# Sets of three dense phases kept in DRAM as high and low parts, and four smaller edits, in a one-core decoder layer

## The chip, the cores and the metric

The kernel runs on one core of a Trainium2 chip. The metric is device microseconds of one execution, the median of three runs. A comparison with another kernel is made on the same chip, and a difference under 0.2% is taken as none that could be told from noise.

The core has five engines that the text names: PE (matmul, with its weight loads PEld), DVE (elementwise, reads PSUM), ACT (elementwise and the activation functions, reads PSUM), POOL (elementwise, on SBUF alone) and SP, which issues DMAs. Each engine works off its own list in order, so an instruction that waits holds up all that stands behind it. POOL and ACT can issue DMAs too.

## The reference

One layer of a decoder trunk on x of 2048 tokens by 1024 channels, float32:

```python
mod = silu(c) @ w_ada + b_ada;  shift, scale, gate = split(mod, 3)
u = x * (1 + scale) + shift
q, k, v, a_gate, p_in, p_gate, m_a, m_p = split(u @ w_in)
a = sliding_window_sink_attention(q, k, v) * silu(a_gate) @ w_attn_proj      # 16 heads, window 128
p = group_linear(multiscale_causal_pool(p_in)) * pool_scale * silu(p_gate) @ w_pool_proj
y = (sigmoid(m_a) * a + sigmoid(m_p) * p) @ w_out * (1 + gate)
out = layer_norm(ALPHA * x + y) * ln_gain + ln_bias
```

The pool takes means over the last 2, 4, 8 or 16 tokens, by channel group, less the token itself. Dense products make up nearly all of the arithmetic.

## The kernel before, in words

**Dense products.** Every large product is done with seven block products in place of eight (a Strassen-like scheme on 2 x 2 blocks). A `Quad` (line 226) is a pair of weight tiles with its consumer; `front` (299) and `back` (309) run the seven products of a quad. The moving operand is a *set*: seven named blocks `B11, T1, T2, B21, T3, B22, T4` (and `B12`, which replaces `T2` once the quads are done). To get float32 precision, each operand is split into a high part `hi` (fp32r, a copy by ACT) and a low part `lo = x - hi` (a subtraction by DVE, helper `low`, line 122), and each 128x128 by 128x512 block takes three matmuls (`mm3`), so one product is 12 matmuls. A set tile in SBUF holds `[hi, lo]`, 2 MB for each name. The weights of a quad pass through `W` tiles (2 buffers): POOL forms their sums (lines 240 to 250), ACT and DVE split them (`pair_split` 270, `half_split` 276) into `w_set` tiles (4 buffers).

**Stages, in order.** (1) `head` (941): the modulation vectors, and the sets of u for the first 1024 tokens. (2) `first_phase` (1032): the product with w_in (k, v and the four gates, 17 quads in 9 groups), with side work between the products: folding of the pool weights, spreading of the relative bias, and the sums that make the sets of u for the other 1024 tokens (`sums_to` 189). (3) `attention` (555) for the first half, 64 steps plus a tail; a step computes scores, softmax, transposes and values of two heads by 128 queries, and 12 matmuls of the q or pool projection stand between. (4) `second_phase` (1065): as (2) for the second half; its side work makes the sets of w_out. (5) attention for the second half. (6) the dense phases `attn, pool, attn, pool` of the two halves and then `out` with the layer norm.

**Where sets come from.** `set_store` (109) keeps the blocks of a set in DRAM as plain float32. `build` (181) loads half a block to a `spare` tile and splits it with ACT and DVE into the set; `PLAN` (379) and `planned` (384) say at which position of a dense phase each build stands, the last ten halves of the next phase's set in the last group of the phase before it. At the end of an attention (from step 57 on, `spots`, line 695) sixteen quarter blocks of B11, T2, B21 and B22 of the next dense phase are loaded (`raw`) and split; T1 came earlier (steps 26 to 45). After an attention T3 and T4 are built at once.

**Order.** `ring` (350) calls `tick` after each product; `steps` (369) puts side work at numbered ticks. Instructions that are issued through `pe, act, dve, pool, sp` (class `Ordered`, line 49) stay behind whatever was written before them on their engine. Those issued through `nc.<engine>` are placed by a planner that knows only estimated costs and arrival times. Attention's loop is ordered by hand but for its loads; head, side work and the dense products are left to the planner.

**Stores of attention.** `finish` (621) multiplies an output tile with its gate on POOL, forms the sums T1 to T4 there, and `put` (186) stores each by a DMA that POOL issues. `pool_diff` (614) writes the pool difference by DVE to a tile `pl` with one buffer, which POOL then reads.

Of the kernel before, what the change touches and what calls it, by code (L numbers as in the profile page):

```python
# [18 lines left out]
P = 128  # L19
# [3 lines left out]
CH = 512  # L23
# [35 lines left out]
def kernel(  # L59
# [52 lines left out]
    u_d = [set_store(f"u{s}") for s in range(2)]  # L112
    wo_d = set_store("wo")
# [67 lines left out]
    def build(ph, name, half, store, source=None):  # L181
        r = ph.spare()
        nc.sync.dma_start(r, store[source or name][half].rearrange("p a b -> p (a b)"))
        split_set(name, 2 * half, r.rearrange("p (a b) -> p a b", a=2), 2)

    def put(store, name, i, src):
        nc.gpsimd.dma_start(store[name][i // 2, :, i % 2, :], src)

    def sums_to(store, i, take, load, work, b12, stretch):

        b = []

        def x(r, c):
            return b[r][:, c * CH : (c + 1) * CH]

        def fetch():
            b.extend((take(), take()))
            for r in range(2):
                load(b[r], r)

        def sub(out, a, c):
            nc.gpsimd.tensor_tensor(x(*out), x(*a), x(*c), ALU.subtract)

        def plain():
            for r in range(2):
                for c in range(2):
                    if b12 or (r, c) != (0, 1):
                        put(store, f"B{r + 1}{c + 1}", i, x(r, c))

        return [  # L210
            (stretch * at, f)
            for at, f in (
                (0, fetch),
                (2, lambda: [work(t, r) for r, t in enumerate(b)]),
                (3, plain),
                (7, lambda: sub((0, 1), (0, 1), (0, 0))),
                (8, lambda: (put(store, "T1", i, x(0, 1)), sub((1, 1), (1, 1), (0, 1)))),
                (9, lambda: (put(store, "T2", i, x(1, 1)), sub((1, 0), (1, 0), (1, 1)))),
                (10, lambda: (put(store, "T4", i, x(1, 0)), sub((0, 0), (1, 1), (0, 0)))),
                (11, lambda: put(store, "T3", i, x(0, 0))),  # L220
            )
        ]
# [3 lines left out]
    class Quad:  # L226
# [7 lines left out]
        def load(self, ph, own):  # L234
            self.w, self.a22 = ph.weights(), ph.last(own)
            x = self.w
            nc.sync.dma_start(x[:, 2, :], self.srcs[1][:, 0:CH])
            nc.sync.dma_start(self.a22, self.srcs[1][:, CH:])
            nc.sync.dma_start(x[:, 0, :], self.srcs[0][:, 0:CH])
            nc.gpsimd.tensor_tensor(x[:, 1, :], x[:, 2, :], self.a22, ALU.add)  # L240

        def mid(self):
            x = self.w
            nc.gpsimd.tensor_tensor(x[:, 1, :], x[:, 1, :], x[:, 0, :], ALU.subtract)  # L244
            nc.gpsimd.tensor_tensor(x[:, 2, :], x[:, 0, :], x[:, 2, :], ALU.subtract)  # L245
            nc.sync.dma_start(x[:, 0, :], self.srcs[0][:, CH:])
# [23 lines left out]
    def pair_split(ph, raw):  # L270
        hi, lo = ph.split(), ph.split()
        nc.scalar.copy(by_two(hi), raw)  # L272
        low(nc.vector, by_two(lo), raw, by_two(hi))
        return halves(hi, lo)
# [109 lines left out]
    def planned(hooks, ph, store, last, skip=()):  # L384
        for p, name, half in PLAN:
            if name in skip or (p < 14) != last:
                continue
            key = (-1, p) if last else (0, p - 14)
            hooks.setdefault(key, []).append(lambda name=name, half=half: build(ph, name, half, store))
# [116 lines left out]
    def bias_rows(ph):  # L506
        rel = ph.t.tile([HEADS, BUCKETS], F32, tag="c", bufs=ph.bufs["c"], name="rel")
        nc.scalar.dma_start(rel, relT)
# [15 lines left out]
    def spread_bias(j):  # L524
        nc.scalar.dma_start(e_rep[:, 2 * j : 2 * j + 2, :], e_d[2 * j : 2 * j + 2, :].partition_broadcast(P))
# [29 lines left out]
    def attention(ph, s, q0, nxt):  # L555
# [4 lines left out]
        def ld(name, src, x=None):  # L560
            x = tp.tile([P, CH], F32, tag="ld", bufs=3, name=name) if x is None else x
            nc.sync.dma_start(x, src)
            return x

        def from_bias(name):
            return tp.tile([P, CH], F32, tag="bt", bufs=2, name=name)
# [30 lines left out]
        def pool_sums(m, t, acc):  # L597
# [7 lines left out]
            while k < w:  # L605
                nx = tp.tile([P, 16 + CH], F32, tag="nxt", bufs=2, name="nxt")
# [7 lines left out]
        def pool_diff(m, cur, acc):  # L614
            pl = tp.tile([P, CH], F32, tag="pl", bufs=1, name="pl")
            dve.scalar_tensor_tensor(pl, cur[:, 16:], 1.0 / POOL_W[m // 2], acc, ALU.mult, ALU.subtract)
            return pl

        kept = {}

        def finish(kind, store, m, t, src, gate):
# [4 lines left out]
            if (half, t) == (0, 0):  # L626
                put(store, "B11", i, x)
                return
            if (half, t) == (0, 1):
                pool.tensor_tensor(x, x, kept[kind, 0, 0], ALU.subtract)  # L630
                put(store, "T1", i, x)
                return
            if (half, t) == (1, 0):
                put(store, "B21", i, x)
                return
            put(store, "B22", i, x)
            b11, t1, b21 = kept[kind, 0, 0], kept[kind, 0, 1], kept[kind, 1, 0]
            pool.tensor_tensor(t1, x, t1, ALU.subtract)
            put(store, "T2", i, t1)
            pool.tensor_tensor(b21, b21, t1, ALU.subtract)  # L640
            put(store, "T4", i, b21)
            pool.tensor_tensor(b11, t1, b11, ALU.subtract)
            put(store, "T3", i, b11)
# [51 lines left out]
        spots = {57: (0,), 58: (1, 2), 59: (3,), 60: (4, 5), 61: (6,), 62: (7, 8), 63: (9,), 64: (10, 11), 65: (12, 13), 66: (14,), 67: (15,)}  # L695
        raws, pre = {}, {}

        def spot(x):
            return ("B11", "T2", "B21", "B22")[x // 4], x % 4
# [6 lines left out]
        def early_lo(x, which):  # L706
            hi, lo = pre[x, which]
            low(dve if x or which else pool, by_two(lo), nxt_group[x].first(), by_two(hi))
            (nxt_group[x].late if which else nxt_group[x].mid)()
# [499 lines left out]
```

## Time and profile before

| | |
|---|---|
| median of 3 runs | 1950.37 us (1948.66 to 1953.11) |
| the profiled execution, its own time | 1956.69 us |
| its span, first to last instruction | 1954.6 us |
| PE busy | 1767.0 us (90%) |
| DVE, POOL, ACT busy | 1332.4, 1036.4, 940.2 us |
| mean granted TensorE clock | 0.964 |
| DMA | 320.5 MB, 164 GB/s on average |

The profiled execution lies 0.3% above the median. PE is the engine to watch: with nothing in its way one product of 12 matmuls takes 2.72 us, so time in which PE is idle, or runs at a lower clock, is what can be won or lost. Rows of the trace read: start, duration, engine, line, operation, output <- inputs, count, and in brackets the idle time before with what ended it. In a group's row the last part is the busy time, the mean of one in ns, and the idle time before. SPq, POOLq and ACTq are DMA issues.

### The profile page before, as it was taken

The page shows a single profiled execution, that of the slowest core. Times are in us where ns is not written, and L with a number is a line of the kernel's source. Part 1 is how long each engine was busy: PE and PEld are TensorE (multiplying, and loading weights), DVE is VectorE, ACT ScalarE, POOL GpSimd, SP SyncE. Part 2 cuts the span into 40 slices and gives each one's busy share as a digit, 9 for nine tenths or more (in the row PEclk, how much of TensorE's full clock was granted, in tenths as well). Part 3 has the DMA queues.
Part 4 walks back from the last instruction along what each step waited for, and adds up shares of the span by engine and source line. Part 5 has one row for each costly group of instructions (what it writes and reads, how often), then busy time and mean ns, then how long its engine had stood idle before and what let it go on. Part 6 is the DMA issues. An engine that isn't in the chain of part 4 may idle for free. (4 is left out here: it accounts for less than half of the span.)

```text
span 1954.6 us, 25013 instructions
## 1 busy us (share of the span) xinstructions
PE 1767.0 (90%) x8248; PEld 1457.9 (75%) x8248; DVE 1332.4 (68%) x2226; ACT 940.2 (48%) x1945; POOL 1036.4 (53%) x902
## 2 busy tenths in 40 slices
PE   3789898999999987989999999999779989989996
PEld 3677777778888876767888888887657768767775
DVE  4775756444787778666543467866877897878776
ACT  2533333334777766523333377776634333333443
POOL 5453545451467677665433136567753764566442
PEclk9789999999999999989999999999889999999998
DMA  7463636464344444564332425443466575675432
GB/s 265 182 204 108 221 124 221 142 203 135 114 151 146 141 140 160 192 206 158 123 120 102 153 86 157 135 141 124 145 226 218 187 246 173 221 241 180 139 137 91
DMA packets 134226, 320.48 MB, mean 164 GB/s; under 512 B 17857, under 2 KB 21969, under 8 KB 134097
## 3 DMA queue, kind: packets, MB, share of 16 engines
q1 hardware_dynamic: 109472, 242.80, 38.5%
q0 software_dynamic: 19232, 62.95, 8.4%
q10 hardware_dynamic: 5392, 13.14, 1.9%
q8 instruction: 65, 1.06, 0.2%
q14 instruction: 65, 0.52, 0.1%
HBM read 213.94 MB, written 108.03 MB: 165 GB/s over the span
## 5 line engine op out<-in xcount | busy, mean ns | idle before, releaser
L55 PE MATMUL mm<-set_B,w_set 128*128 128x512 f32 x3240 | 814.9, 401 | 32.5 <-DVE w_set L123 17.5
L55 PEld LDWEIGHTS mm<-set_B,w_set 128*128 128x128 f32 x3240 | 613.5, 192 | 166.5 <-DVE w_set L123 23.5
L55 PE MATMUL lg<-set_T,w_set 128*128 128x512 f32 x2088 | 535.9, 407 | 69.1 <-DVE w_set L123 31.6
L55 PEld LDWEIGHTS lg<-set_T,w_set 128*128 128x128 f32 x2088 | 402.2, 196 | 178.1 <-DVE w_set L123 46.8
L123 DVE TENSOR_TENSOR w_set<-W,w_set 128x1024 fp32r<-128x1024 f32 x166 | 238.8, 1438 | 168.8 <-ACT w_set L272 164.7
L272 ACT CAST w_set<-W 128x1024 fp32r<-128x1024 f32 x166 | 174.0, 1048 | 269.1 <-PE mm L55 188.2
L55 PE MATMUL mm<-set_T,w_set 128*128 128x512 f32 x1080 | 271.6, 400 | 0.0
L55 PEld LDWEIGHTS mm<-set_T,w_set 128*128 128x128 f32 x1080 | 205.7, 193 | 43.1
L250 POOL TENSOR_TENSOR W<-W 128x512 f32<-128x512 f32 x58 | 79.6, 1373 | 177.3 <-DVE w_set L123 167.0
L244 POOL TENSOR_TENSOR W<-W 128x512 f32<-128x512 f32 x58 | 95.9, 1654 | 146.6 <-DVE w_set L123 130.6
L323 POOL TENSOR_TENSOR p<-p,u 128x512 f32<-128x512 f32 x58 | 85.8, 1482 | 104.5 <-DVE u L322 104.3
L55 ACT ACTIVATE L<-L,nm 128x257 f32<-128x257 f32 (+1 forms) x256 | 127.1, 498 | 7.9 <-DVE nm L55 2.8
L55 DVE TENSOR_TENSOR o<-pv,o 64x128 f32<-64x128 f32 x256 | 71.9, 281 | 79.4 <-ACT o L55 76.8
L240 POOL TENSOR_TENSOR W<-W,A 128x512 f32<-128x512 f32 x58 | 85.6, 1475 | 63.1 <-DMA W<-in_win_dram 20.9
L55 DVE CUSTOM_DVE_ANT_0 L<-lg,bt,nsink 128x256 f32<-128x256 f32 (+1 forms) x256 | 111.6, 473 | 5.3 <-PE lg L55 1.3
L55 ACT ACTIVATE L<-L,sm 128x256 f32<-128x256 f32 (+1 forms) x128 | 64.3, 502 | 81.2 <-DVE sm L55 81.2
L245 POOL TENSOR_TENSOR W<-W 128x512 f32<-128x512 f32 x58 | 93.4, 1611 | 9.9 <-DMA W<-in_win_dram 3.8
L55 POOL TENSOR_TENSOR w_set<-W,w_set 128x1024 fp32r<-128x1024 f32 x16 | 38.4, 2402 | 102.4 <-ACT w_set L55 69.3
L55 PE MATMUL pv<-pth,vv 128*128 128x256 f32 x248 | 69.6, 297 | 25.5 <-ACT pth L55 21.7
L123 DVE TENSOR_TENSOR w_set<-A,w_set 128x512 fp32r<-128x512 f32 x58 | 86.1, 1516 | 5.4 <-ACT w_set L279 5.3
L123 DVE TENSOR_TENSOR set_T<-spare,set_T 128x1024 fp32r<-128x1024 f32 (+1 forms) x48 | 67.0, 1398 | 32.8 <-ACT set_T L178 32.5
L55 DVE TENSOR_SCALAR L<-L,sm 128x256 f32<-128x256 f32 (+1 forms) x128 | 87.6, 684 | 0.0
(174 smaller groups left out, 2577.3 us busy)
## 6 DMA issues: line engine op xcount, KB each, us to landing
W<-in_win_dram SPq DMA_DIRECT2D x102, 256.0 KB, 3.5
w_set<-wmix_d SPq DMA_DIRECT2D x32, 512.0 KB, 5.5
A<-in_win_dram SPq DMA_DIRECT2D x34, 256.0 KB, 3.8
ag_d<-sig SPq DMA_DIRECT2D x32, 256.0 KB, 3.4
pg_d<-sig SPq DMA_DIRECT2D x32, 256.0 KB, 3.3
ma_d<-sig SPq DMA_DIRECT2D x32, 256.0 KB, 2.6
mp_d<-sig SPq DMA_DIRECT2D x32, 256.0 KB, 2.9
ag<-ag_d SPq DMA_DIRECT2D x32, 256.0 KB, 2.8
```

Source lines behind the costliest of these rows:

```text
L55: return lambda *args, **kw: self.tc.keep_in_program_order(op(*args, **kw))
L123: engine.tensor_tensor(dst, src, as32(hi), ALU.subtract)
L240: nc.gpsimd.tensor_tensor(x[:, 1, :], x[:, 2, :], self.a22, ALU.add)
L244: nc.gpsimd.tensor_tensor(x[:, 1, :], x[:, 1, :], x[:, 0, :], ALU.subtract)
L245: nc.gpsimd.tensor_tensor(x[:, 2, :], x[:, 0, :], x[:, 2, :], ALU.subtract)
L250: nc.gpsimd.tensor_tensor(x[:, 0, :], x[:, 0, :], x[:, 1, :], ALU.subtract)
L272: nc.scalar.copy(by_two(hi), raw)
L323: nc.gpsimd.tensor_tensor(p5, p5, u2, ALU.add)
```

## The change

What it does, part by part:

1. Three set stores, `u1` (u of the second half), `wo` (w_out) and `ain0` (attention output of the first half), hold each block as its high and low part (`split_store`, 2 MB for a name in place of 1 MB). Side work makes the parts: `kept_parts` copies by ACT, subtracts by DVE into two `c` tiles (5 buffers, shared with the gates' `sig` and others) and stores both by SP. `sums_to` does this for u1 (32 times, in `first_phase`) and wo (28 times, in `second_phase`); its POOL subtractions stand 1.5 ticks apart. `resplit` reads the 14 halves that attention stored plainly for `ain0`, splits them (28 times) and stores the parts again, in `second_phase`. Attention of the second half still stores plain blocks, and so does the pool.
2. Where these sets are used, `fill_set` loads a half (1 MB) by one DMA into the set, with no split: T1 in attention at steps 26 and 42, B11, B21, T2 and B22 at steps 57, 58, 59 and 61, T3 and T4 at the start of the next phase, and all fourteen halves of the out phase.
3. The head is written out in a fixed order on all engines. Loads of a tile stand a stage ahead, the spreading of the bias and the folding are ordered at their ticks, and the sets T3, T4 and B22 of the last two blocks are made inside the first phase (`rest`).
4. `pool_diff` writes in place of the pool's sum; the `nxt` tiles have three buffers, and the difference and its gate's multiplication stand one step earlier.
5. Attention's stores are issued by SP, one step after they were called for (`later`).

The diff, cut to its core:

```diff
+    def split_store(name):
+        return {n: dp.tile([4, P, 2, CH], F32, name=f"{name}_{n}_split") for n in set_names}
+    b12_d = dp.tile([2, P, 2, CH], F32, name="b12_d")
+    u1_d = split_store("u1")
+    wo_d = split_store("wo")
+    ain0_d = split_store("ain0")
...
+    def fill_set(name, half, src, eng=None):
+        dst = as32(sets[name][:, 2 * half : 2 * half + 2])
+        (eng or nc.sync).dma_start(dst, src[2 * half : 2 * half + 2].rearrange("i p h c -> p i h c"))
+
     def put(store, name, i, src):
-        nc.gpsimd.dma_start(store[name][i // 2, :, i % 2, :], src)
+        sp.dma_start(store[name][i // 2, :, i % 2, :], src)
+
+    def kept_parts(ph, dst, src):
+        t = []
+        def split():
+            t.extend(ph.c(n, F32R) for n in ("k_hi", "k_lo"))
+            act.copy(t[0], src())
+            low(dve, t[1], src(), t[0])
+        def keep():
+            for h in range(2):
+                sp.dma_start(dst[:, h, :], as32(t[h]))
+        return split, keep
...
+        todo = [(0, fetch), (3, lambda: work(b[0], 0)), (3.5, lambda: work(b[1], 1))]
+        todo += [(at, sub(*z)) for at, z in (
+            (7.5, ((0, 1), (0, 1), (0, 0))), (9, ((1, 1), (1, 1), (0, 1))),
+            (10.5, ((1, 0), (1, 0), (1, 1))), (12, ((0, 0), (1, 1), (0, 0))))]
+        for at, name, z in (
+            (4, "B11", (0, 0)), (4.7, "B12", (0, 1)), (5.4, "B21", (1, 0)), (6.1, "B22", (1, 1)),
+            (8.5, "T1", (0, 1)), (10, "T2", (1, 1)), (11.5, "T4", (1, 0)), (13, "T3", (0, 0)),
+        ):
+            if b12 or name != "B12":
+                split, keep = kept_parts(ph, store[name][i], lambda z=z: x(*z))
+                todo += [(at, split), (at + 1, keep)]
+        return sorted(todo, key=lambda t: t[0])
+
+    def resplit(ph, name, half):
+        r = []
+        def fetch():
+            r.append(ph.spare())
+            sp.dma_start(r[0], ain_d[0][name][half].rearrange("p a b -> p (a b)"))
+        todo = [(0, fetch)]
+        for j in range(2):
+            split, keep = kept_parts(ph, ain0_d[name][2 * half + j], lambda j=j: r[0][:, j * CH : (j + 1) * CH])
+            todo += [(3 + j, split), (4 + j, keep)]
+        return todo
...
         def pool_diff(m, cur, acc):
-            pl = tp.tile([P, CH], F32, tag="pl", bufs=1, name="pl")
-            dve.scalar_tensor_tensor(pl, cur[:, 16:], 1.0 / POOL_W[m // 2], acc, ALU.mult, ALU.subtract)
+            pl = cur[:, 16:]
+            dve.scalar_tensor_tensor(pl, pl, 1.0 / POOL_W[m // 2], acc, ALU.mult, ALU.subtract)
...
+            for what in puts:
+                put(*what)
+            puts.clear()
...
+            if n in (59, 62):
+                nxt_group[n // 62].mid()
...
             if n in (26, 42):
-                t1_raw = ph.weights()[:, 0:2]
-                nc.sync.dma_start(t1_raw, nxt_store["T1"][n // 42])
-            if n in (29, 45):
-                split_set("T1", 2 * (n // 45), t1_raw, 2, eng=(act, pool))
+                fill_set("T1", n // 42, nxt_store["T1"], sp)
+            for start, name in ((57, "B11"), (58, "B21"), (59, "T2"), (61, "B22")):
+                if n == start:
+                    for half in range(2):
+                        fill_set(name, half, nxt_store[name], sp)
...
-            for x in spots.get(n, ()):
-                name, i = spot(x)
-                split_set(name, i, raws.pop(x), eng=(act, dve))
...
+        load_w(0)
+        load_x(0)
+        load_w(4)
+        load_x(4)
+        for q in grp:
+            q.load(ph, False, sp, pool)
+        load_w(1)
+        modulation(0)
+        load_x(1)
+        sets_a(0)
...
+        products(2)
+        sets_a(3)
+        sets_b(3)
+        products(3)
+        return groups, turn, opened, cb, lambda: (sets_c(2), sets_c(3))
...
-            steps(hooks, groups, 9 + 24.5 * i, todo)
+            steps(hooks, groups, 5 + 26.5 * i, todo)
+            for n in range(4):
+                if halves_of:
+                    steps(hooks, groups, 19 + 26.5 * i + 2.6 * n, resplit(ph, *halves_of.pop(0)))
...
-                    hooks.setdefault((0, p), []).append(lambda name=name, half=half: build(ph, name, half, ain_d[0]))
+                    hooks.setdefault((0, p), []).append(lambda name=name, half=half: fill_set(name, half, ain0_d[name]))
```

In the head, `sets_a(i)` makes B11 and T1 of block i, `sets_b(i)` B21 and T2, `sets_c(i)` B22, T3 and T4; `load_w` and `load_x` issue the loads of the modulation's weights and of x, and `products(i)` are the first 12 matmuls on block i.

More of the change, by code (lines that the diff above doesn't have):

```diff
@@ L201, in sub @@
         def sub(out, a, c):
[L202 to L222, printed above, removed]
+            return lambda: pool.tensor_tensor(x(*out), x(*a), x(*c), ALU.subtract)
+        todo = [(0, fetch), (3, lambda: work(b[0], 0)), (3.5, lambda: work(b[1], 1))]
+        todo += [(at, sub(*z)) for at, z in (
+            (7.5, ((0, 1), (0, 1), (0, 0))),
+            (9, ((1, 1), (1, 1), (0, 1))),
+            (10.5, ((1, 0), (1, 0), (1, 1))),
+            (12, ((0, 0), (1, 1), (0, 0))),
+        )]
+        for at, name, z in (
[16 more added lines that the diff above has]
+        return todo
     class Quad:
@@ L626, in finish @@
             if (half, t) == (0, 0):
-                put(store, "B11", i, x)
+                later(store, "B11", i, x)
                 return
@@ L694, in attention @@
         seconds = {}
[L695 to L699, printed above, removed]
+        pre = {}
         def early_hi(x, which):
@@ L1010, in head @@
-        groups, turn = gate_quads(0)
-        fetch(0)
-        fetch(4)
-        for q in groups[0]:
-            q.load(ph, False)
-        starts = [pair_split(ph, q.first()) for q in groups[0]]
-        for q in groups[0]:
-            q.mid()
-        opened = [(bank(), bank(), None, None) for q in groups[0]]
-        for i in range(4):
-            make_sets(i)
-            if i + 1 < 4:
-                fetch(i + 1)
-                fetch(i + 5)
+                act.activation(x, x, AF.Identity, bias=mod[:, k : k + 1], scale=mod[:, m : m + 1])
@@ L1024, in head, with products @@
+        opened = [(bank(), bank(), None, None) for q in grp]
+        def products(i):
             for w, (a, b, _, _) in zip(starts, opened):
```

275 lines of the change are left out of this document (157 added, 118 removed).

## The prediction

> **What bounds the kernel now.** I read the page's head first, then busy time by stage, then the chain of waits of PE in the stages with a gap, and at last the timeline there. Columns of the second fence: stretch in us, its length, PE, PEld, DVE, ACT and POOL busy, granted clock, DMA share, GB/s.
>
> ```profile
> span 1954.6 us, 25013 instructions
> PE 1767.0 (90%) x8248; PEld 1457.9 (75%) x8248; DVE 1332.4 (68%) x2226; ACT 940.2 (48%) x1945; POOL 1036.4 (53%) x902
> ```
>
> ```profile
> 0.00:85.00 85.00, 43.45 (x176) 37.68 (x176) 49.76 (x90) 33.67 (x49) 45.63 (x66) 0.89 0.68 239
> 85.00:480.00 395.00, 366.01 (x1626) 298.05 (x1627) 222.10 (x237) 143.07 (x207) 174.23 (x159) 0.96 0.51 172
> 480.00:700.00 220.00, 217.60 (x1240) 189.86 (x1240) 169.18 (x508) 165.75 (x499) 132.18 (x127) 1.00 0.41 131
> 700.00:778.00 78.00, 61.08 (x292) 48.66 (x291) 60.28 (x134) 46.69 (x123) 57.69 (x53) 0.91 0.45 149
> 778.00:960.00 182.00, 165.06 (x679) 132.75 (x680) 121.78 (x118) 67.85 (x97) 106.89 (x93) 0.94 0.52 176
> 960.00:1125.00 165.00, 165.00 (x730) 136.67 (x729) 69.80 (x76) 61.27 (x87) 50.88 (x36) 1.00 0.38 126
> 1125.00:1340.00 215.00, 212.97 (x1219) 186.15 (x1218) 158.91 (x488) 162.87 (x479) 124.37 (x115) 1.00 0.41 130
> 1340.00:1439.00 99.00, 71.36 (x351) 57.68 (x350) 69.17 (x154) 54.45 (x146) 70.53 (x64) 0.89 0.46 152
> 1700.00:1790.00 90.00, 77.14 (x312) 59.43 (x311) 74.43 (x59) 31.39 (x37) 62.17 (x48) 0.96 0.71 234
> ```
>
> PE bounds the kernel: in the middle of both attentions and in 960-1125 it has next to no idle time and a clock of 1.00, so nothing done there for another engine can pay. Length less PE busy gives the idle time that the change can reach: head 41.6 us, first phase 29.0, end of the first attention 16.9, second phase 16.9 (all of it before 960), end of the second attention 27.6, start of the out phase 12.9.
>
> **The head (part 3).**
>
> ```profile
> 28.91 1.53 DVE L123 TENSOR_TENSOR set_T<-b,set_T 128x512 fp32r<-128x512 f32 x1
> 41.17 1.24 ACT L992 ACTIVATE spare<-spare,mod 128x1024 f32<-128x1024 f32 x1 [10.20 <-DMA spare<-in_xt_dram]
> e_rep<-e_d ACTq DMA_DIRECT2D x8, 384.0 KB, 5.9
> spare<-in_xt_dram SPq DMA_DIRECT2D x5, 512.0 KB, 6.9
> ```
>
> Block 0's sets end at 30.4 and ACT waits 10.2 us for block 1's x; its DMAs stood behind others on SP, and eight spreads of the bias ran on ACT's queue meanwhile. In the new order block 1's x is among the first loads and the spreads come at later ticks: -10 us. The splits moved to `rest` lie beside the first products of `back`, which has its own T2 and B21 by then. The fixed order costs something where a load waits: `load_x(2)` needs the `spare` that `sets_c(0)` frees, and the loads of blocks 6 and 3 stand behind it on SP. The trace has no such wait, so I bound it by one landing of 6.9 us at each of blocks 1 to 3, which is 21 us; against it stands at most the 10.2 and one spread (5.9). **Head: -10** (-16 to +11), near the row because the order names the very load that it waited for.
>
> **The ends of the attentions (parts 2, 4, 5).** The first fence groups DVE's work in 1340-1439, the second has waits of PE in 1340-1400 and in 1400-1450, the third is the timeline with two groups of POOL's.
>
> ```profile
> L55 DVE TENSOR_TENSOR set_B<-raw,set_B 128x512 fp32r<-128x512 f32 x12 | 15.7, 1320 | 4.6 <-ACT set_B L55 4.5
> L55 DVE TENSOR_TENSOR set_T<-raw,set_T 128x512 fp32r<-128x512 f32 x4 | 5.1, 1284 | 2.9 <-ACT set_T L55 2.9
> L55 DVE SCALAR_TENSOR_TENSOR pl<-nxt,mm 128x512 f32<-128x512 f32 x4 | 2.7, 683 | 10.1 <-POOL p L55 8.8 <-POOL nxt L55 1.2
> ```
>
> ```profile
> PE pv L55 <- ACT pth L55: 8.6, 3, 6.8
> PE mm L55 <- ACT u L313: 9.3, 1, 9.3
> ```
>
> ```profile
> 1359.04 0.57 POOL L187 DMA_DIRECT2D ain_T<-a  x1 [2.88 <-issue]
> 1369.93 0.69 DVE L55 SCALAR_TENSOR_TENSOR pl<-nxt,mm 128x512 f32<-128x512 f32 x1 [8.84 <-POOL p L55]
> 1371.89 0.58 PE L55 MATMUL pv<-pth,vv 128*128 128x256 f32 x1 [6.83 <-ACT pth L55]
> 1378.74 0.28 PE L55 MATMUL pv<-pth,vv 128*128 128x256 f32 x1
> 1438.04 0.58 ACT L313 COPY u<-mm 128x512 f32<-128x512 f32 x1 [8.67 <-DMA ain_T<-a]
> L187 POOL DMA_DIRECT2D ain_T<-a x32 | 18.1, 566 | 14.0 <-POOL a L55 8.6 <-issue 5.1 <-PE mm L55 0.3
> L187 POOL DMA_DIRECT2D pin_T<-p x32 | 18.0, 563 | 9.5 <-POOL p L55 8.0 <-PE pv L55 0.9 <-PE pt L55 0.3
> ```
>
> Three things hold PE. Sixteen splits take 20.8 us of DVE and 7.5 us of waiting for their casts, inside DVE's softmax list; by loading halves ready they go. The single `pl` buffer makes DVE wait 8.8 us for a late POOL, and softmax, transposes and PE (6.83) wait behind it; written in place, that wait is gone, and what is late next is the pool's sum itself (1.2 us here). POOL is late because it issues the stores: the two rows are 64 of the 112 that the code issues, with 36.1 us busy and 23.5 idle ahead, so some 0.9 us each, 52 us of POOL an attention, which SP takes over at no cost to PE as long as POOL is in time. The last wait, 9.3 us, is `back`'s copy waiting for a store of `a` to land before its memory is reused; without splits and stores ahead of it POOL's last four products come sooner, but a tail stays.
>
> What it costs: SP waits for POOL at each store, with bias tiles, q weights and gates queued behind it. Weights are loaded four steps ahead of use, but a pool gate is now used one step after its load. Fills are 8 DMAs of 1 MB; the stretch 1700-1790 moves 234 GB/s at a share of 0.71, so 330 at full share, 25 us for all. From step 57 to the end of the tail are eleven steps of some 4.2 us (1219 matmuls at 24 a step in 215 us), so B22 is in time; a gate queued behind two fills is 6 us late. Of 44.5 us idle I leave 7 for each end and count nothing for the clock: **-30**. Bounds: all idle but 2 each and the lost clock, -42; only `pl` and a third of the rest, -12.
>
> On the clock: after the 6.83 us gap the same matmul took 0.58 us, later 0.28. [...]
>
> **The out phase (part 2).**
>
> ```profile
> L123 DVE TENSOR_TENSOR set_T<-spare,set_T 128x1024 fp32r<-128x1024 f32 x8 | 12.9, 1615 | 10.0 <-ACT set_T L178 10.0
> L123 DVE TENSOR_TENSOR set_B<-spare,set_B 128x1024 fp32r<-128x1024 f32 x6 | 11.7, 1996 | 0.2 <-ACT set_B L178 0.2
> PE lg L55 <- DVE w_set L123: 6.1, 3, 3.4
> PE lg L55 <- DVE w_set L123: 4.3, 3, 3.4
> ```
>
> All fourteen builds of w_out stand in 1700-1790: 24.6 of DVE's 74.4 us, and the two rows (1700-1750 and 1750-1800) show PE waiting for weights split late on that DVE. As fills they cost DMA alone, 7 MB more at a share of 0.71, which is the risk. Half of the 12.9 us idle: **-6** (-12 to 0).
>
> **The two gate phases (parts 1, 2, 3).** What goes:
>
> ```profile
> 830.43 1.23 DVE L1088 TENSOR_TENSOR spare<-spare,cb 128x1024 f32<-128x1024 f32 x1 [9.04 <-DMA spare<-in_wout_dram]
> DVE spare L1088 <- DMA spare<-in_wout_dram: 16.5, 5, 9.0
> PE lg L55 <- DVE p L334: 4.2, 1, 4.2
> 212.47 6.83 DVE L123 TENSOR_TENSOR w_set<-A,w_set 128x512 fp32r<-128x512 f32 x2
> L1079 SPq DMA_DIRECT2D spare<-in_wout_dram x16: 327/394/433, 792.6 to 876.6; - x16
> ```
>
> The planner put w_out's side work into 790-900, as early as it could, where DVE waited 16.5 us for its loads with weight splits behind it. In 150-250, as in each round of `sums_to`, PE waits 4.2 us because two splits took 6.83 us together, while POOL had a run of subtractions and stores back to back. The new ticks spread the subtractions, keep stores off POOL and leave each load three ticks (8 us). I take 30 of the 45.9 us idle in the two phases as gone.
>
> What comes: 32 + 28 + 28 = 88 more splits of 128x512, one cast and one subtraction each; 190 more DMAs on SP at 0.39 us (176 stores, 14 loads), which is 74 us of SP in 742, before W's loads in the list; and 28 MB more in the second phase. DVE is busy 55% there and takes some 60 us more, so it has room. The question is what stands behind a split. A steady stretch:
>
> ```profile
> 1003.95 1.05 ACT L272 CAST w_set<-W 128x1024 fp32r<-128x1024 f32 x1 [3.89 <-PE mm L55]
> 1005.03 1.23 DVE L123 TENSOR_TENSOR w_set<-W,w_set 128x1024 fp32r<-128x1024 f32 x1 [2.94 <-ACT w_set L272]
> 1006.64 2.88 PE L55 MATMUL mm<-set_B,w_set 128*128 128x512 f32 x12
> ```
>
> The weight split can only begin when PE frees its buffer, and it is ready 0.38 us before PE wants it. A foreign subtraction just ahead of it, 1.3 us as in the `raw` rows, costs PE 0.9; one placed behind it falls into DVE's gap of 2.9 us and costs none. Traced behind the weight's split of the same tick, most fall into the gap: I take 0.3 us for each, 26 us in all (ends 0 and 0.9). T3 and T4 at the start of the second phase and of the first dense phase come by fills, where their builds lay beside waits already counted. **Sum of both phases: -30 + 26 = -4** (-30 to +49).
>
> **The sum.** -10 - 30 - 6 - 4 = -50. The profiled execution took 1956.69 us (span 1954.6) and lies 6.3 above the median of 1950.37. So 1906.7 for that execution and, the terms being stalls that every run has, **1900** against the median, -2.6%.
>
> **The rivals.** *Slower: weight splits queued behind side splits.* If the 88 meet the 0.38 us of slack badly, and DVE's wait comes on top of ACT's cast (0.6 us), each costs 0.9 to 1.5 us; at 1.2 the two phases stand at -30 + 106, and with -46 from the other terms the time is 1980. It decides from (46 + 30) / 88 = 0.86 us a split. For it: PE runs with no idle in 960-1125 because no side work is there, and now there is. Against it: side splits in 85-480 are of the same kind (folding) and leave 29 us idle in 395.
>
> What speaks for it beyond the slack is the row of 6.83 us: DVE's subtraction from SBUF, 0.68 at its fastest, waits out POOL. [...]
>
> *The attentions give a third.* Gates queued behind the fills, POOL a step late for the earlier difference, or SP held by a store: the wait moves from `p` to `nxt` or to a DMA. At -12 in place of -30: 1918. For it: the 1.2 us of `nxt` and the one-step gate. Against: POOL sheds 52 us.
>
> *All covers hold.* Side splits cost nothing (-30), the attentions give -40, the head -12, out -8: 1860.
>
> *It does nothing*: gains at the ends and losses in the gate phases cancel, -46 against some +46; that needs just the 0.86 us, and has little room.
>
> **How the numbers follow.** Likeliest 0.50, 1900 with its own range 1880 to 1912; a third 0.18; all covers 0.12; slower rival 0.17; no change 0.03. Faster 0.80, same 0.03 (within 0.2%, about what a measurement can tell), slower 0.17. The range leaves out the slow rival alone: 1860 to 1948.
>
> **What would show it.** Block 1's x with no 10 us wait; no `pl` waiting on `p`, no set splits and no POOL store in the attentions, with PE idle 7 us at each end; no set splits in the out phase's start; idle PE spread thinly over 960-1125 where there was none. I am wrong if PE's waits for `w_set` in the gate phases grow past 80 us, if SP's stores make W loads land late, or if DVE waits for the pool's sums or gates.

## The result, and the profile after

The changed kernel takes 1899.6 us (1890.62 to 1900.92) against 1950.9 for the kernel before: a ratio of 0.9727, interval 0.9695 to 0.9759. Run again beside the experiments it gave 0.9746 (0.9724 to 0.9768). The forecast was 1900.

The head of the page after, and then busy time by stage (stretch in us, its length, PE, PEld, DVE, ACT and POOL busy, granted clock, DMA share, GB/s):

```profile
span 1897.2 us, 25359 instructions
PE 1748.8 (92%) x8248; PEld 1446.6 (76%) x8248; DVE 1301.5 (69%) x2261; ACT 942.3 (50%) x1974; POOL 923.7 (49%) x724
```

```profile
76.70:105.00 28.30, 16.87 (x74) 12.74 (x72) 18.91 (x20) 13.41 (x22) 14.79 (x14) 0.82 0.25 86
476.00:680.00 204.00, 202.98 (x1153) 176.27 (x1152) 150.55 (x473) 151.64 (x459) 99.48 (x82) 1.00 0.43 140
680.00:757.00 77.00, 71.92 (x380) 61.68 (x379) 53.93 (x155) 51.45 (x149) 52.73 (x44) 0.93 0.62 225
940.00:1104.00 164.00, 159.45 (x698) 130.33 (x697) 92.83 (x101) 70.06 (x107) 64.06 (x42) 1.00 0.71 251
1104.00:1320.00 216.00, 215.02 (x1227) 187.17 (x1226) 157.94 (x496) 163.37 (x484) 103.04 (x79) 1.00 0.42 138
1320.00:1389.00 69.00, 61.52 (x337) 52.20 (x335) 47.00 (x131) 42.11 (x121) 51.17 (x41) 0.97 0.63 233
```

The same 8248 matmuls; POOL has 178 instructions less, DVE and ACT a few more. The two stretches at the ends of the attentions (680 to 757 and 1320 to 1389) leave PE idle for 5.1 and 7.5 us, where it was 16.9 and 27.6, and their clocks are 0.93 and 0.97 in place of 0.91 and 0.89. The middle of the second phase (940 to 1104), which had no idle time, now has 4.6 us of it.

One table serves the result and the experiments. It has the length of each stage in us in the profiled execution, from the timeline: the head ends with the first `sig<-mm` on ACT, the first phase with the first score on PE, an attention with the first long run of `mm<-set_B` matmuls after it (24, of which a trace can miss a few), the second phase with the first `L<-L,sm` on ACT, the dense stage with ACT's first pass over `wide`.

| kernel | head | first phase | attention 0 | second phase | attention 1 | dense | out | span | ratio to before |
|---|---|---|---|---|---|---|---|---|---|
| before | 104.7 | 375.8 | 297.9 | 352.7 | 307.6 | 361.1 | 154.8 | 1954.6 | 1 |
| after | 104.8 | 371.6 | 280.6 | 352.0 | 280.6 | 353.9 | 153.7 | 1897.2 | 0.9727 |
| after again (e5) | 103.9 | 374.5 | 281.2 | 358.0 | 282.3 | 356.7 | 153.3 | 1909.8 | 0.9746 |
| e1 rest late | 95.5 | 379.0 | 281.6 | 357.4 | 282.6 | 354.2 | 153.3 | 1903.6 | 0.9699 |
| e2 no resplit | 103.6 | 375.9 | 279.9 | 340.9 | 283.9 | 354.1 | 154.6 | 1892.8 | 0.9695 |
| e3 stores on POOL | 105.4 | 368.4 | 285.1 | 357.4 | 293.1 | 355.4 | 154.4 | 1919.2 | 0.9822 |
| e4 pl of its own | 103.5 | 375.5 | 279.9 | 354.3 | 280.4 | 353.6 | 152.8 | 1900.0 | 0.9721 |
| e6 splits and loads | 104.7 | 369.6 | 302.3 | 354.9 | 303.7 | 355.8 | 154.2 | 1945.3 | 0.9982 |
| e7 before, SP's stores | 104.2 | 373.7 | 287.1 | 357.0 | 291.8 | 361.2 | 155.3 | 1930.2 | 0.9883 |
| e8 gate columns | 96.8 | 397.9 | 279.9 | 354.5 | 280.7 | 355.7 | 153.4 | 1918.9 | 0.9844 |
| e9 before, pl in place | 106.0 | 371.5 | 292.7 | 350.5 | 302.5 | 361.3 | 153.1 | 1937.6 | 0.9941 |
| e10 splits, no loads | 105.3 | 369.2 | 287.8 | 353.1 | 292.6 | 354.4 | 153.3 | 1915.7 | 0.9838 |
| e11 gate late | 95.9 | 369.1 | 280.7 | 353.9 | 281.8 | 354.9 | 152.8 | 1889.1 | 0.9679 |
| e12 e7 and e9 together | 105.1 | 374.5 | 285.6 | 356.6 | 290.0 | 363.1 | 154.5 | 1929.4 | 0.9871 |

Each row is one profiled execution; those of e1 and e5 were the slowest of their five. Where the code of a stage is the same, its length differs by up to 4 us from its mean in the two gate phases (the first and the second phase) and by 2 in an attention, so a single row says nothing finer. Means over the rows with equal code, changed less before: head -0.5, first phase -1.8, attentions -42.9 (605.5, of which there is one row, to 562.6), second phase +0.9, dense -6.8, out -0.8. They add up to -51.9, beside 51 by the medians. Most of the gain lies in the attentions, and there at the ends: the stretches in their middle had next to no idle time before.

### The profile page after: what moved, and what is told of

The parts are those of the page before. It is cut to its first block, busy times and chain, and to the rows that moved or that the text cites. A ratio compares the mean times of both kernels' runs of the same rounds, so it can differ in the third digit from the quotient of the medians.

```text
span 1897.2 us, 25359 instructions
## 1 busy us (share of the span) xinstructions
PE 1748.8 (92%) x8248; PEld 1446.6 (76%) x8248; DVE 1301.5 (69%) x2261; ACT 942.3 (50%) x1974; POOL 923.7 (49%) x724
## 5 line engine op out<-in xcount | busy, mean ns | idle before, releaser
L55 PE MATMUL lg<-set_T,w_set 128*128 128x512 f32 x2088 | 527.7, 402 | 59.2 <-DVE w_set L128 24.6
L55 PEld LDWEIGHTS lg<-set_T,w_set 128*128 128x128 f32 x2088 | 397.4, 193 | 166.7 <-DVE w_set L128 39.0
L128 DVE TENSOR_TENSOR w_set<-W,w_set 128x1024 fp32r<-128x1024 f32 x164 | 236.1, 1439 | 99.3 <-ACT w_set L307 89.7
L285 POOL TENSOR_TENSOR W<-W 128x512 f32<-128x512 f32 x58 | 79.9, 1377 | 169.1 <-DVE w_set L128 164.5
L279 POOL TENSOR_TENSOR W<-W 128x512 f32<-128x512 f32 x56 | 88.0, 1571 | 142.7 <-DVE w_set L128 122.9
L55 DVE TENSOR_TENSOR k_lo<-spare,k_hi 128x512 fp32r<-128x512 f32 x88 | 83.9, 957 | 65.6 <-ACT k_hi L55 31.9
L275 POOL TENSOR_TENSOR W<-W,A 128x512 f32<-128x512 f32 x56 | 80.0, 1429 | 87.6 <-DMA W<-in_win_dram 23.8
L55 POOL TENSOR_TENSOR w_set<-W,w_set 128x1024 fp32r<-128x1024 f32 x14 | 33.7, 2408 | 146.5 <-ACT w_set L55 108.5
L280 POOL TENSOR_TENSOR W<-W 128x512 f32<-128x512 f32 x56 | 90.9, 1623 | 22.9 <-DMA W<-in_win_dram 19.7
L55 POOL TENSOR_TENSOR p<-nxt,pg 128x512 f32<-128x512 f32 x32 | 41.3, 1292 | 123.2 <-DVE sm L55 113.6
L55 ACT COPY o<-pv 64x256 f32<-64x256 f32 x128 | 47.2, 369 | 80.6 <-PE pv L55 76.4
L55 DVE TENSOR_TENSOR ptl<-pt,pth 128x512 fp32r<-128x512 f32 (+1 forms) x128 | 85.6, 669 | 1.7 <-ACT pth L55 1.6
L55 ACT CAST k_hi<-spare 128x512 fp32r<-128x512 f32 x88 | 53.9, 616 | 60.3 <-POOL spare L55 29.7
```

Source lines behind the costliest of these rows:

```text
L55: return lambda *args, **kw: self.tc.keep_in_program_order(op(*args, **kw))
L128: engine.tensor_tensor(dst, src, as32(hi), ALU.subtract)
L275: e.tensor_tensor(x[:, 1, :], x[:, 2, :], self.a22, ALU.add)
L279: e.tensor_tensor(x[:, 1, :], x[:, 1, :], x[:, 0, :], ALU.subtract)
L280: e.tensor_tensor(x[:, 2, :], x[:, 0, :], x[:, 2, :], ALU.subtract)
L285: nc.gpsimd.tensor_tensor(x[:, 0, :], x[:, 0, :], x[:, 1, :], ALU.subtract)
```

## The head gave nothing: e1, e8, e11

The first T2 product on PE starts at 76.73 us (85.45 before), so the new order did bring the head forward by 9 us; but PE then stops. Timeline of the changed kernel, rows of PE, DVE and POOL:

```profile
76.73 0.61 PE L55 MATMUL lg<-set_T,w_set 128*128 128x512 f32 x2
92.80 1.22 PE L55 MATMUL lg<-set_T,w_set 128*128 128x512 f32 x2 [9.78 <-ACT w_set L307]
81.91 4.12 DVE L55 TENSOR_TENSOR set_T<-spare,set_T 128x512 fp32r<-128x512 f32 x1 [0.82 <-ACT set_T L55]
85.96 0.68 DVE L55 TENSOR_TENSOR set_T<-b,set_T 128x512 fp32r<-128x512 f32 x1
79.92 1.30 POOL L55 TENSOR_TENSOR spare<-A,spare 128x512 f32<-128x512 f32 x1
81.17 1.30 POOL L55 TENSOR_TENSOR b<-b,A 128x512 f32<-128x512 f32 x1
82.99 1.27 POOL L55 TENSOR_TENSOR spare<-A,spare 128x512 f32<-128x512 f32 x1
84.21 1.27 POOL L55 TENSOR_TENSOR b<-b,A 128x512 f32<-128x512 f32 x1
```

The weight split that PE waits for 9.78 us stands on ACT and DVE behind `rest`, the six casts and subtractions for B22, T3 and T4 of blocks 2 and 3, and behind the first group's fold. One of these subtractions, 0.68 us by itself, took 4.12: it ended 0.55 us after the last of POOL's four sums. Why it waited for them is not shown. e1 moved `rest`, and the first group's fold and sums with it, two ticks on:

```diff
-        at(0, 0, rest)
+        at(0, 2, rest)
-            steps(hooks, groups, 28 * g, fold_parts(ph, g))
+            steps(hooks, groups, 28 * g + (0 if g else 2), fold_parts(ph, g))
-            steps(hooks, groups, 28 * i + 5, todo)
+            steps(hooks, groups, 28 * i + (5 if i else 7), todo)
```

> The changed kernel with the sets of the head's last two blocks (B22, T3, T4) made behind the weight split of the second quad, at tick 2 in place of tick 0; the first folding and the first sums move two ticks to make room. Theory (the head's gain is lost because the second quad's weight split stands behind these six splits on ACT): PE's gap of 9.8 us at 83 us shrinks to 3 or less, the first attention's scores start 6 to 8 us earlier (476 becomes 468 to 470), time about 1893, ratio to the kernel before 0.969. Rival (PE waits there for the sets themselves, T3 above all): the gap moves to the first T3 product with the same length, scores start at 474 to 478, time 1898 to 1901.

Measured: 0.9699 (0.9677 to 0.9722), 5 to 9 us under the changed kernel by its two ratios, and a head of 95.5 us. So the reading of the gap holds: no wait of PE between 70 and 470 us is longer than 5.3 us now, so it didn't move to a T3 product, though the rival's times (first scores at 474 to 478, 1898 to 1901 us) are the ones that came. For the first score starts at 474.5, where the theory had 468 to 470: in this execution, the slowest of five, some 7 of the 9 us were gone by the end of the first phase. The timeline of e1 there, and its DMAs from 430 to 460 (KB each, median us to landing):

```profile
452.49 1.04 ACT L183 CAST set_T<-spare 128x1024 fp32r<-128x1024 f32 x1 [10.54 <-DMA spare<-b_d]
454.63 1.22 PE L55 MATMUL lg<-set_T,w_set 128*128 128x512 f32 x2 [5.34 <-ACT w_set L314]
```

```profile
q10 hardware_dynamic: 1040, 0.00, 1.9%
W<-in_win_dram SPq DMA_DIRECT2D x2, 512.0 KB, 8.4
spare<-b_d SPq DMA_DIRECT2D x2, 512.0 KB, 9.4
gate_d<-mod ACTq DMA_DIRECT2D x1, 4.0 KB, 15.1
```

ACT waits 10.5 us for one half of T2, one of the two loads `spare<-b_d`, with PE's next weights behind it. In the same 30 us runs `gate_d<-mod`, the transposed store of the gates: 4 KB in 1024 pieces of 4 B. Its line belongs to the second phase, but this DMA isn't among those that the kernel holds to program order, and it is issued as soon as the last gate modulation is done (a row of sums on DVE, which writes `mod`; in the changed kernel the last ends at 444.32 us and the issue is at 444.35). e8, on top of e1's edit, wrote it column by column:

```diff
+        def put():
+            k = m - 2 * KT
+            nc.scalar.dma_start(gate_d[k : k + 1].rearrange("k p -> p k"), mod[:, m : m + 1], ...)
-        return (0, fetch), (3, work)
+        return (0, fetch), (3, lambda: (work(), put()))
...
-            nc.scalar.dma_start(gate_d.rearrange("k p -> p k"), mod[:, 16:24], ...)
```

> The changed kernel with the late split of blocks 2 and 3 of before-last run e1 (rest two ticks later) and with the gates' 1024 four-byte pieces written column by column, each after its own gate product, in place of one transfer of 15 us whose landing the load of T2 (10.5 us late for ACT) waited beside. Theory: the 9 us that the head gained in e1 were lost again at the end of the first phase behind that transfer; without it the first scores start at 466 to 471 us and the time is 5 to 9 us below the changed kernel's. Rival: the load of T2 was late from the weights' own traffic: first scores at 473 to 477, time within 3 us of the changed kernel's.

Measured: 0.9844 (0.9824 to 0.9864), some 19 us slower than the changed kernel; the first score comes at 494.7. The cure was wrong, and the landing times say more than the theory did. DMAs of e8 from 105 to 465, and two of ACT's waits there (in total, times, longest):

```profile
spare<-b_d SPq DMA_DIRECT2D x2, 512.0 KB, 13.5
mr<-in_mix_dram SPq DMA_DIRECT2D x3, 256.0 KB, 8.3
gate_d<-mod ACTq DMA_DIRECT2D x8, 0.5 KB, 9.5
```

```profile
ACT w_set L307 <- DMA W<-in_win_dram: 10.8, 3, 8.2
ACT w_set L307 <- DVE mod L55: 8.2, 1, 8.2
```

An eighth of the pieces still takes 9.5 us to land, so eight such transfers are worse than one; loads that fall beside them are late (13.5 and 8.3 us, where e11 below has 4.2 and 3.8), and ACT, which issues them, once stood 8.2 us waiting for the `mod` that DVE writes. e11, also on top of e1's edit, keeps one transfer and moves it instead, held to program order, to step 6 of the first attention:

```diff
+            if n == 6 and s == 0:
+                act.dma_start(gate_d.rearrange("k p -> p k"), mod[:, 16:24], ...)
...
-            nc.scalar.dma_start(gate_d.rearrange("k p -> p k"), mod[:, 16:24], ...)
```

> e1 (the late split two ticks on) with the gates' 1024 four-byte pieces sent in one transfer, as in the changed kernel, but at step 6 of the first attention and not at the end of the first phase. Theory: that transfer stood before the landing of T2's load (14.3 us in e1); with it gone the load lands in 5 to 8 us, PE's wait of 5.3 us at the end of the phase goes, first scores at 466 to 471 us, ratio 0.965 to 0.969. Rival: T2's load is late from the weights' own traffic: first scores at 473 to 477, ratio 0.969 to 0.973.

Measured: 1890.94 us, ratio 0.9679 (0.9659 to 0.9699), the lowest of all runs; the first score comes at 465.0, a little before the range. DMAs of e11 from 105 to 465:

```profile
W<-in_win_dram SPq DMA_DIRECT2D x2, 512.0 KB, 3.6
spare<-b_d SPq DMA_DIRECT2D x2, 512.0 KB, 4.2
```

The T2 loads land in 4.2 us where they took 9.4, and PE's 5.3 us are gone. That the gates' transfer held up its neighbours is shown; how it does is not, for its packets fill 1.9% of the DMA engines' time. What moving it is worth in the whole time isn't settled: the profiles differ by 9.9 us in the first phase, but by the ratios e11 is 0.2% below e1, and their intervals overlap. Both edits together are worth 9 to 13 us by the two ratios of the changed kernel.

## The attentions: e3, e4, e6, e7, e9, e10, e12

Three large things were changed at the ends: the stores went from POOL to SP, the pool difference goes in place, and 16 splits went. Each was undone in the changed kernel, and the first two were made alone in the kernel before. Smaller edits of the loop were not tried alone: T1's split (on ACT and POOL) went, the difference and its gate stand a step earlier, and the next weights' sums moved to steps 59 and 62.

```diff
-        sp.dma_start(store[name][i // 2, :, i % 2, :], src)
+        nc.gpsimd.dma_start(store[name][i // 2, :, i % 2, :], src)
...
-            puts.append(what)
+            put(*what)
```

> The changed kernel with attention's 112 stores issued by POOL again, at once, as in the kernel before. Theory (splits, the one pl buffer and POOL's stores each hold a part, and POOL with 52 us more an attention is late only at the ends): the two attentions together 6 us longer, 3 to 12, time about 1905. Rival one (the stores were the root, the other two only passed POOL's lateness on): 25 us or more longer, 1925. Rival two (POOL has room without them): within 2 us.

Measured for e3: 0.9822 (0.9802 to 0.9841); the attentions take 578.2 us, 15.6 more than the 562.6 of the changed kernel. The theory's 6 falls, and the rival's 25 is not reached.

```diff
-            pl = cur[:, 16:]
-            dve.scalar_tensor_tensor(pl, pl, ...)
+            pl = tp.tile([P, CH], F32, tag="pl", bufs=1, name="pl")
+            dve.scalar_tensor_tensor(pl, cur[:, 16:], ...)
```

> The changed kernel with the pool difference written to a tile of its own with one buffer, and two nxt buffers, as in the kernel before; it stays one step earlier. Theory: POOL, freed of its stores, reads the tile soon, so DVE's wait on it stays under 1 us at a time and the attentions are 3 us longer, 0 to 8, time about 1902. Rival (the single buffer was the root of the gaps at the ends, 4.3 and 6.8 us): 12 us or more longer, 1912 and up.

Measured for e4 (with two `nxt` buffers again in place of three): 0.9721 (0.9701 to 0.9742) and 560.3 us of attention. In the changed kernel the buffer is worth nothing that can be seen. Beside the base e5, e6 put the splits back, into a scratch tile, loads and all:

> The changed kernel once more, beside the next three, so that they have their base: 0.9727 of the time before, within 0.9695 to 0.9759, and attentions of 280 us each from the first score to the first product of the next phase.

```diff
...
+            for x in spots.get(n, ()):
+                raw = raws.pop(x)
+                act.copy(scr[:, x % 2], raw)
+                low(dve, scr[:, x % 2], raw, scr[:, x % 2])
+            for x in spots.get(n + 1, ()):
+                name, i = spot(x)
+                raws[x] = ld("raw", nxt_store[name][i, :, 0, :])
...
```

> The changed kernel with 16 splits (a cast and a subtraction of 128x512 each, with the load of their operand) put back at steps 57 to 67 of each attention, into a scratch tile; the sets themselves come ready, as before. Theory now: the stores on POOL were 17 us of the 44 that the attentions lost (4.5 and 12.5 when they were put back), and the 16 splits are the other 27: each attention 10 to 14 us longer, the whole 20 to 28 us slower than the changed kernel, ratio to the kernel before 0.983 to 0.987. Rival: POOL was the root, and the splits lay beside DVE's waits for it: 0 to 3 us an attention, 0 to 6 in all, ratio 0.973 to 0.976.

Measured: e5 0.9746, as expected; e6 0.9982 (0.9967 to 0.9996), 43.4 us more of attention than the mean of the changed kernel, beyond both theories. Waits at the end of e6's second attention (1338 to 1436):

```profile
ACT scr L55 <- DMA raw<-ain_T_split: 11.4, 3, 8.0
ACT scr L55 <- DMA raw<-ain_B_split: 8.9, 5, 3.4
DVE scr L55 <- ACT scr L55: 24.5, 8, 9.9
PE pv L55 <- ACT pth L55: 15.2, 5, 9.1
SPq L55 <- POOL a L55: 25.5, 10, 9.7
```

The operands of the splits came late: their loads stand on SP behind stores that wait for POOL and behind fills of 1 MB, ACT waited 20.3 us for them, DVE behind ACT, and PE behind the softmax. So e6 measured more than splits. e10 takes the splits from keys that lie in SBUF:

```diff
+        any_raw = as32(kk[:, 0, 0, P : P + CH])
...
+            for x in range(spots.get(n, 0)):
+                act.copy(scr[:, x], any_raw)
+                low(dve, scr[:, x], any_raw, scr[:, x])
```

> The changed kernel with the 16 splits of e6 at the same steps, but made from keys that lie in SBUF: casts and subtractions alone, no loads. Theory now: the kernel before with SP's stores still lost 17 us of attention against the changed one, which is what the splits cost, and the other 27 us of e6 were operands loaded late behind stores that wait for POOL: 12 to 20 us slower than the changed kernel, ratio to the kernel before 0.980 to 0.985. Rival: the casts and subtractions themselves stop the softmax: 35 to 45 us, ratio 0.993 to 0.998. Second rival: they cost next to nothing, 0 to 5, and in the kernel before too it was their loads: 0.973 to 0.977.

Measured: 0.9838 (0.9820 to 0.9856), 580.4 us of attention, 17.8 more than the changed kernel. The theory holds: the casts and subtractions cost 18, and the other 26 of e6 came with the loads, whose late landing its waits show. (Both runs also keep their scratch in one of the three `qs` buffers; what that costs wasn't tried alone.) Waits of e10 (1330 to 1410), and below them the like row of e5 (1332 to 1400):

```profile
DVE scr L55 <- ACT scr L55: 6.3, 7, 1.5
ACT L L55 <- DVE sm L55: 15.1, 11, 3.2
```

```profile
ACT L L55 <- DVE sm L55: 3.4, 2, 3.2
```

DVE's softmax list is what the splits lengthen: ACT waits 15.1 us for it in place of 3.4. Now the same from the other end, in the kernel before. e7 moves the stores alone:

```diff
-                put(store, "B11", i, x)
+                later(store, "B11", i, x)
...
+            for what in puts:
+                put_sp(*what)
+            puts.clear()
```

> The kernel before with one edit: the attention's stores issued by SP one step later, splits and pl buffer as they were. Theory now (stores 17, splits 27, the parts add): 14 to 20 us faster than the kernel before, ratio 0.990 to 0.993, no wait of pl on p above 2 us. Rival (POOL is the root): 30 to 44 faster, 0.978 to 0.985. Second rival (the splits hold the ends anyway, so that the stores pay only once the splits are gone): within 5 us, 0.997 to 1.003.

e9 writes the difference in place alone (e4's diff the other way round), and e12 does both:

> The kernel before with one edit: the pool difference written in place into the sums' buffer (three such buffers, no buffer of its own), stores on POOL and splits as they were. Theory now: the waits of DVE on p come from a POOL that is late by its stores, so they go over to nxt at the same length: 0, within 3 us either way, ratio 0.998 to 1.002. Rival, the prediction's reading: the single buffer made the 8.84 us wait at each attention's end, so some 15 us go: ratio 0.992.

> The kernel before with the edits of e7 and e9 together: stores by SP one step later and the pool difference in place; only the 16 splits are left of what the ends of the attentions lost. In the profiles the two attentions took 605.5 us before, 578.9 with the stores moved, 595.2 with pl in place, and 561 to 564 in the changed kernel. Theory: the two edits work on the same wait (DVE on a late POOL), so pl adds little once the stores are gone: 574 to 580 us of attention, ratio 0.984 to 0.989, and the splits' share against the changed kernel is 12 to 18 us, as e10 measured it. Rival: they add: 566 to 571 us, ratio 0.980 to 0.983, and the splits' share is 4 to 9.

Measured: e7 0.9883 (0.9865 to 0.9900), e9 0.9941 (0.9924 to 0.9957), e12 0.9871 (0.9856 to 0.9887). In us of attention: 605.5 before, 578.9 with the stores moved, 595.2 with the difference in place, 575.6 with both. e7 gained a little more than its theory had (23 us by the ratio); e9 (11 or 12 us by the ratio) lies nearer to the prediction's reading than to the newer theory's none; e12 is the theory's: once POOL is in time, the buffer adds 3 by the profiles, and by the ratios nothing clear of noise. Waits of e9 (1330 to 1430) and of e7 (1330 to 1414):

```profile
DVE nxt L55 <- POOL nxt L55: 3.5, 1, 3.5
PE pv L55 <- ACT pth L55: 7.3, 6, 3.1
PE mm L55 <- ACT u L313: 9.0, 1, 9.0
```

```profile
DVE pl L55 <- POOL p L55: 1.2, 1, 1.2
PE pv L55 <- ACT pth L55: 3.4, 2, 2.2
PE mm L55 <- ACT u L316: 6.3, 1, 6.3
ACT set_B L55 <- DMA raw<-ain_B: 3.8, 4, 2.0
```

The 8.84 us of `pl` on `p` shrink to 3.5 of `nxt` by the one edit and to 1.2 by the other: two cures of one wait, and they don't add. (e7's last row bears on e6: there such loads stand behind the same stores, but behind no fills, and ACT waited 3.8 us. The fills are the likely difference; they weren't tried alone.) With both, 30 of the 43 us are accounted for. The remaining 13 are left to the splits and the smaller edits together; that the splits are most of it is argued from e10, where putting them back cost 18.

## The second phase: e2

e2 leaves out the 28 re-splits of the second phase; both parts of the attention output's sets are then filled from the raw values, so their low part is not computed.

```diff
...
-            for n in range(4):
-                if halves_of:
-                    steps(hooks, groups, 19 + 26.5 * i + 2.6 * n, resplit(ph, *halves_of.pop(0)))
...
```

> The changed kernel without the 28 splits, 14 loads and 56 stores that remake the first half's attention output: its sets are filled from the plain store, low part too, so that part of the output is left uncomputed in low precision. The fills move the same bytes. Theory of the prediction (0.3 us of PE a side split): the second phase, from the first product after the attention to the next scores, is 8 us shorter than the changed kernel's, time about 1891. Rival one (side splits stand before weight splits and cost 0.9 to 1.2 us each): 25 to 34 us shorter, about 1870. Rival two (they lie in gaps and cost nothing): within 2 us, 1898 to 1900.

Measured: 0.9695 (0.9671 to 0.9719), which is 6 to 10 us under the changed kernel by the two ratios; in the profile the phase takes 340.9 us beside a mean of 355.1, so 14.2. That is 0.2 to 0.5 us a split, loads and stores included: about the 0.3 that was taken by the ratios, a little dearer if the profile is believed, and below the 0.86 from which the slow rival decides. The 60 other side splits were not taken out. One stretch of the changed kernel, and below it the same of e2:

```profile
900.00:1000.00 100.00, 95.06 (x408) 76.84 (x407) 67.03 (x72) 45.17 (x70) 44.17 (x29) 0.98 0.72 248
```

```profile
900.00:1000.00 100.00, 97.54 (x427) 79.42 (x426) 58.94 (x60) 40.38 (x59) 43.94 (x30) 1.00 0.47 165
```

Without the re-splits PE does 19 matmuls more in 100 us, at a DMA share of 0.47 and not 0.72. Whether the arithmetic or the traffic costs it, e2 doesn't tell, since it takes away both.

## Why the prediction was right

The total was right to a microsecond, and that is luck, for the terms were not: a gain of 10 that didn't come in the head was made up by one that was sized 13 too small in the attentions.

**Head, -10: measured -0.5.** Block 1's x did come sooner, and PE started 9 us earlier. The step that failed is "the splits moved to `rest` lie beside the first products of `back`": they stood ahead of the weight split that these products needed. e1 moved them and had the 9 us.

**Attentions, -30: measured -42.9**, at the far bound that was given (-42). Two of the three parts of the mechanism hold as they were told, the splits and the late POOL; the third, the single `pl` buffer, is a second cure of POOL's lateness and was not needed beside the first. The idle time left was right: 12.6 us where 14 were taken, a gain of 31.9. The mis-sized term is "count nothing for the clock". Busy time over both attentions (480 to 778 with 1125 to 1439 before, 476 to 757 with 1104 to 1389 after):

```profile
sum 612.00, PE 563.02 PEld 482.35 DVE 457.55 ACT 429.77 POOL 384.78; mean PE 281.51 PEld 241.18 DVE 228.77 ACT 214.88 POOL 192.39
```

```profile
sum 566.00, PE 551.44 PEld 477.33 DVE 409.42 ACT 408.56 POOL 306.42; mean PE 275.72 PEld 238.66 DVE 204.71 ACT 204.28 POOL 153.21
```

PE was busy 11.6 us less, for 3099 and 3093 recorded matmuls (the six are about 1 us of it): the same products run faster, at the higher clock that the stretches at the ends show now that their gaps are small (0.93 and 0.97 for 0.91 and 0.89, with 5.1 and 7.5 us idle for 16.9 and 27.6). The bound of -42 holds 40.5 us of idle time (44.5 less 2 at each end) and so some 1.5 for the lost clock, the author's estimate, which no run shows; the profiles show these 11.6 in its place. The rival in which the attentions give a third did not come: at the ends PE's longest waits are 3.6 us (values, for DVE's `o`) and 4.0 (the tail that was foreseen, on a store of `a`), and none is for gates or fills.

**Out phase, -6: measured -7.6** over dense and out; 6.8 of it lies ahead of the first pass over `wide`, where the builds of w_out stood. PE's waits in 1700 to 1800 of the kernel before, and in 1640 to 1760 of the changed kernel:

```profile
PE lg L55 <- DVE w_set L123: 7.0, 5, 3.4
PE mm L55 <- DVE w_set L123: 3.7, 3, 2.8
```

```profile
PE mm L55 <- DVE w_set L128: 6.2, 3, 4.2
PE lg L55 <- DVE w_set L128: 1.3, 2, 0.7
```

The waits for weights split on DVE fell from 10.7 to 7.5 us, and the idle time of 90 us at the start of the phase from 12.9 to 7.0: the half that was taken. (The two rows of the prediction, 6.1 and 4.3, both hold the wait of 3.4 at 1749 us.) No run undid these fills alone, so the cause is argued from the waits.

**Gate phases, -4: measured -0.9**, within what single rows can tell. The two terms in it, -30 and +26, weren't measured apart: PE's idle time over both phases is 43.4 us in the changed kernel's profile where it was 42.7, and e2 prices 28 of the 88 splits. Idle time is now spread thinly over 940 to 1104, as the prediction said it would be. The slow rival fell on its price. What spoke for it is there:

```profile
L55 DVE TENSOR_TENSOR k_lo<-spare,k_hi 128x512 fp32r<-128x512 f32 x88 | 83.9, 957 | 65.6 <-ACT k_hi L55 31.9 <-DMA pg_d<-sig 7.6 <-DMA ag_d<-sig 4.7
```

The 88 new subtractions took 0.957 us on the mean and 0.676 at the fastest, and 31 of them took more than 0.75. Each of these 31 ended 0.55 us after the end of an elementwise operation of POOL, as the 4.12 us one in the head did. So these 31 do wait out POOL, though no row shows why. But in e2 PE paid 0.5 us a split at the most, below the 0.86 from which that rival decides.

## What to carry to other kernels

Work that is moved "beside" an engine's products has to be placed behind the operation that these products wait for next, on every engine that it uses, in the queue's order and not by the sum of busy times. Two edits that shorten the same wait need not add, so undo each alone and make each alone before saying what it was worth. When long gaps of PE go, count the slower matmuls behind them too (0.58 us for one of 0.28 behind the gap of 6.83 us): here that was a quarter of the attentions' gain.

## What the runs showed of the hardware that was not expected

A transposed store of 4 KB in 4-byte pieces takes 15.1 us to land and holds up loads of 512 KB that run beside it (9.4 in place of 4.2 us), at 1.9% of the DMA engines' time; an eighth of it, 0.5 KB, still takes 9.5. The queue that carried it shows 1040 packets in e1's 30 us, about one for each of its 1024 pieces. And DMAs that a kernel doesn't hold to program order can be issued hundreds of us before their place: in the changed kernel this one was issued at 444 us, and the load of the next line, which reads what it wrote, at 753. Last, the 31 long subtractions above (`k_lo<-spare,k_hi`): what takes DVE 0.68 us at its fastest took up to 1.78, and the like one in the head 4.12, and each ended 0.55 us after an operation of POOL.
